# Attention of a hybrid encoder layer with TensorE's order written out: the sink as a column of the score tile, outputs in a PSUM bank of their own, memory rows in two tiles

## The chip, the cores and the metric

The kernel runs on one core of a Trainium2 chip. The core has five engines that each work through a queue of their own in order: TensorE (PE, matmuls; its weight loads appear as a row of their own, PEld), VectorE (DVE), ScalarE (ACT), GpSimd (POOL) and SyncE (SP, which here only issues DMAs). Matmul results go to PSUM, eight banks of 512 fp32 columns on 128 partitions; everything else is in SBUF. The metric is the device time in microseconds (us) of one execution, the median of several runs.

## The reference

One layer of a hybrid encoder, 1024 tokens, model width 1024, all in fp32. One projection of the normalised input feeds a windowed attention and a state-space branch (SSD); both are projected back, weighted by sigmoid gates, summed and projected once more; a cross-attention into 256 memory rows and a squared-ReLU MLP follow.

```python
def reference(x, mem, ...):
    h = rmsnorm(x, norm_mix)
    proj = h @ w_in                      # q, k, v, z, xbc, dt, gate_a, gate_b
    attn = windowed_gqa_sink(q, k, v, attn_sink)
    ssd = ssd_branch(z, xbc, dt_raw, ...)
    merged = sigmoid(gate_a) * (attn @ w_attn_branch) + sigmoid(gate_b) * (ssd @ w_ssd_branch)
    x = x + merged @ w_out
    h = rmsnorm(x, norm_cross)
    x = x + cross_attention(h, rmsnorm(mem, norm_mem), w_xq, w_xkv, w_xo)
    h = rmsnorm(x, norm_ffn)
    x = x + square(relu(h @ w_up)) @ w_down
    return rmsnorm(x, norm_final)

def windowed_gqa_sink(q, k, v, sink):    # 16 heads of 64 over 4 kv heads, blocks of 128 queries
    # each block sees its own and both neighbouring blocks of keys
    s = einsum('bnqgrd,bnkgd->bngrqk', qb, kw) * d ** -0.5 + bias   # ALiBi, -inf outside |t-s| <= 128
    m = maximum(max(s, axis=-1), sink)
    p = exp(s - m)
    denom = sum(p, axis=-1) + exp(sink - m)
    return einsum('bngrqk,bnkgd->bnqgrd', p / denom, vw)
```

## The kernel before

**Products.** An fp32 operand is split into a high and a low part of a format that PE multiplies faster. A product then takes three matmuls (`mm3`, lines 83, 87 and 88): high by high, high by low, low by high. A weight tile is loaded to `raw` by a DMA on SP, its high part `whi` copied by ACT (L64), its low part `wlo` subtracted by POOL (L67). Where a product's result is itself an operand of the next, ACT copies the high part out of PSUM and DVE subtracts the low one.

**Stages.** `phase0` normalises the rows and projects the memory rows; `ssd_phase` runs to about 904 us; `attn_phase` to 1227 us; `merge_phase` projects both branches, beginning with the last gate block (END_GATE, 15) whose first matmul is `mps` of L83; cross-attention and the MLP follow. In all stages but attention PE runs in the order in which the code issues its matmuls (`manual_schedule`). In `attn_phase` a list scheduler of the framework orders every engine, PE too.

**Attention.** For each of four kv heads (`kv`): a key projection of two heads at once in every second round (`kps`, 48 matmuls of 512 columns), in the first round also the values (`vp`, 192 matmuls of 256 columns, L694 to L708), the query projections (`qps`, two units of 48), then eight query blocks (`qb`). `scores(qb)` (L747 to L775) takes for each of four heads `i` two matmuls (`sps`, L761 and L762) over 256 or 384 keys; DVE adds the bias and keeps the minimum, in `t` and `nm` (L763; scores are held negated). Four short operations on [128, 4] tiles deal with the sink: `nm` is lowered to the negated sink (L765), `es` = `nm` + sink (L766), its exp on ACT (L767), and after the four exps of the scores (L769, which also sum into `den`) `den` + `es` (L771). DVE takes the reciprocal (L772), POOL normalises `t` (L774). `values(qb, t4)` (L777 to L802) turns the normalised scores by PE transposes, 4 for each of two or three key blocks (`pt`, L784), splits them into `ph` on ACT (L787) and `pl` on DVE (L788), and multiplies by the values (`op`, L793 and L794, four or six matmuls). ACT copies both halves out (`oa` L797, `ob` L798), POOL adds them (L799), SP stores the sum to `d_at` (L801). `scores` is issued two blocks ahead of `values`. After the blocks of a kv head its gate blocks (`gps`, `ATT_GATES`, numbers 11 to 14) are issued.

**PSUM.** From attention on there are two banks for the projections (tag `g`, pool `pg2`) and six (tag `p`, pool `pp6`) that `vp`, `sps`, `pt` and `op` share in turn.

**Phase 0, memory rows.** PE turns the two groups of 128 memory rows in two halves each (`nt`, L189); DVE multiplies each half by the norm's gain into one tile `mT` (L191); the key products `kxp` (L207) and value products read `mT`. The gain spread over the partitions (`gb`, two matmuls) stands ahead of the transposes.

Of the kernel before, what the change touches and what calls it, by code (L numbers as in the profile page):

```python
# [16 lines left out]
P = 128  # L17
S = 1024
D = 1024
NT = 8  # L20
# [9 lines left out]
ATT_GATES = ((), (11,), (12,), (13, 14))  # L30
# [132 lines left out]
def phase0(kx, ins, dr):  # L163
    nc, tc = kx.nc, kx.tc
    V, A, PE = nc.vector, nc.scalar, nc.tensor
    with tc.tile_pool(name="p0", bufs=1, side="right") as p0, tc.manual_schedule(engines={mybir.EngineType.PE}):
# [15 lines left out]
        mT = p0.tile([P, NK, 256], F32, name="mT")  # L182

        def mem_turn(xt, off):
            for kh in range(2):
                ps = kx.pp.tile([P, 512], F32, tag="p", name="nt")
                for j in range(4):
                    k = 4 * kh + j
                    PE.transpose(ps[:, j * P:(j + 1) * P], xt[:, k * P:(k + 1) * P], kx.ident)  # L189
                to = mT[:, 4 * kh:4 * kh + 4, off:off + P]  # L190
                turned = V.tensor_tensor(to, ps.rearrange("p (k c) -> p k c", k=4),  # L191
                                         gm[:, 4 * kh:4 * kh + 4].unsqueeze(2).broadcast_to([P, 4, P]), ALU.mult)
# [10 lines left out]
        def kx_unit(w, j):  # L203
            ps = kx.pp.tile([P, 512], F32, tag="p", name="kxp")[:, :256]
            wv = w.rearrange("p (k c) -> p k c", k=NK)
            for k in range(NK):
                PE.matmul(ps, wv[:, k], mT[:, k], start=k == 0, stop=k == NK - 1)  # L207
# [4 lines left out]
        def vx_unit(ws, c, j):  # L212
            ps = kx.pp.tile([P, 512], F32, tag="p", name="vxp")[:, :256]
            for k in range(NK):
                wv = ws[k // 4].rearrange("p (k c) -> p k c", k=4)
                PE.matmul(ps, mT[:, k, j * P:(j + 1) * P], wv[:, k % 4], start=k == 0, stop=k == NK - 1)
# [459 lines left out]
def attn_phase(kx, ins, dr):  # L676
    nc, tc = kx.nc, kx.tc
    V, A, G, PE = nc.vector, nc.scalar, nc.gpsimd, nc.tensor
    with tc.tile_pool(name="p2", bufs=1) as ap, tc.tile_pool(name="p2r", bufs=1, side="right") as aq:
# [8 lines left out]
        snk = ap.tile([P, 2, 16], F32, name="snk")  # L688
        nc.sync.dma_start(snk[:, 0], ins["sink"].partition_broadcast(P))
        V.tensor_scalar(snk[:, 1], snk[:, 0], -1.0, None, ALU.mult)  # L690

        vhl = ap.tile([P, NT, 4, 2, 64], F32R, name="vhl")

        def v_part():  # L694
            vw = [wload(kx, ins["wv"][kh]) for kh in range(2)]
            vws = wsplit(vw[0], 4) + wsplit(vw[1], 4)
            for b in range(4):
                vp = kx.pp.tile([P, 512], F32, tag="p", name="vp")
                for j in range(2):
                    t = 2 * b + j  # L700
                    for k in range(NK):
                        mm3(kx, vp[:, j * 256:(j + 1) * 256],
                            act_pair(kx.hT[t // 4], k, slice((t % 4) * P, (t % 4) * P + P)),
                            vws[k], k == 0, k == NK - 1)
                vv = slice(2 * b, 2 * b + 2)
                vp2 = vp.rearrange("p (c v q) -> p c v q", c=2, v=4)
                A.activation(vhl[:, vv, :, 0], vp2, AF.Copy)
                V.tensor_tensor(vhl[:, vv, :, 1], vp2, vhl[:, vv, :, 0].bitcast(F32), ALU.subtract)  # L708

        kd = {}  # L710
        for kv in range(4):
            if kv % 2 == 0:
                w = wload(kx, ins["wk"][kv // 2])
                for s in range(2):
                    kd[kv + s] = [aq.tile([P, S], F32R, tag=n, bufs=2, name=n) for n in ("kh", "kl")]
                for h in range(2):
                    ps = kx.pg.tile([P, 512], F32, tag="g", name="kps")
                    gemm_fm(kx, ps, w, kx.hT[h])
                    hs = slice(h * 512, (h + 1) * 512)
                    for s in range(2):  # L720
                        kh, kl = (t[:, hs] for t in kd[kv + s])
                        own, oth = slice(64 * s, 64 * s + 64), slice(64 - 64 * s, 128 - 64 * s)
                        A.activation(kh[own], ps[own], AF.Copy)
                        A.activation(kh[oth], ps[own], AF.Copy)
                        V.tensor_tensor(kl[own], ps[own], kh[own].bitcast(F32), ALU.subtract)
                        V.tensor_tensor(kl[oth], ps[own], kh[own].bitcast(F32), ALU.subtract)
            if kv == 0:
                v_part()
            qs, bias = [], []
            for i in range(4):  # L730
                bt = ap.tile([P, 384], F32, tag="bias", bufs=5, name="bias")
                A.activation(bt, rel, AF.Copy, scale=SLOPES[4 * kv + i])
                bias.append(bt)
            for i in range(2):
                w = wload(kx, ins["wq"][2 * kv + i])
                q2 = [aq.tile([P, S], F32R, tag="q", bufs=6, name="q") for _ in range(2)]
                for h in range(2):
                    ps = kx.pg.tile([P, 512], F32, tag="g", name="qps")
                    gemm_fm(kx, ps, w, kx.hT[h])
                    for s in range(2):  # L740
                        q = q2[s][:, h * 512:(h + 1) * 512]
                        own, oth = slice(64 * s, 64 * s + 64), slice(64 - 64 * s, 128 - 64 * s)
                        A.activation(q[own], ps[own], AF.Copy, scale=-0.125)
# [1042 lines left out]
```

## Time and profile before

| | |
|---|---|
| time, median of 3 runs | 2340.3 us (2335.47 to 2341.06) |
| the profiled execution | 2340.79 us, its span 2339.0 us |
| granted TensorE clock | 1.0 |
| PE busy over the span | 2301.7 us, 98% |
| PEld, DVE, ACT, POOL busy | 1939.9, 1615.7, 1157.3, 936.8 us |
| bytes moved | 251.04 MB, mean 107 GB/s |

The profile is of one execution. A group of instructions is written as line, engine, operation, output<-inputs. "Idle before" or a wait is time in which an engine had nothing to run, put down to the instruction that released it. A matmul's recorded duration covers its way through the array and overlaps the next matmul's; the distance between two starts is what it costs. PEld rows are the loads of the stationary operand, one for each matmul, which run ahead of the matmuls.

### The profile page before, as it was taken

The numbers are of one execution on the slowest core, as the hardware profiler recorded it, in microseconds if no ns is written. First come the engines' busy times: TensorE is split into PE (matmuls) and PEld (weight loads), VectorE is DVE, ScalarE is ACT, GpSimd is POOL, SyncE is SP. The second block draws the span as 40 slices with busy tenths as digits, with TensorE's granted clock in tenths as the row PEclk, the third lists the DMA queues.
The fourth block names the chain that finished last, engine by engine and source line by source line (L and its number), as shares of the span: only waits on it lengthen the run. The fifth ranks groups of instructions, "written<-read, shape, count | busy, mean of one in ns | idle before, by whom it ended". The sixth has DMA issues, their size and how long they took to land.

```text
span 2339.0 us, 32557 instructions
## 1 busy us (share of the span) xinstructions
PE 2301.7 (98%) x11882; PEld 1939.9 (83%) x11882; DVE 1615.7 (69%) x2578; ACT 1157.3 (49%) x2486; POOL 936.8 (40%) x884
## 2 busy tenths in 40 slices
PE   9999999999999999999999999999999999999998
PEld 7888898988889898877878888888977887788887
DVE  5877666677766764565569887866585456689984
ACT  5455654656555564586775442345453333134342
POOL 2355746566474654453550011115585444100010
PEclk9999999999999999999999999999999999999999
DMA  6222324232242322111135257112353345812301
GB/s 231 83 81 91 116 67 125 71 110 85 79 125 66 118 81 83 44 40 54 37 116 209 82 181 260 46 35 66 128 172 120 108 140 168 297 76 89 119 28 72
DMA packets 150322, 251.04 MB, mean 107 GB/s; under 512 B 11409, under 2 KB 86289, under 8 KB 150162
## 3 DMA queue, kind: packets, MB, share of 16 engines
q1 hardware_dynamic: 79408, 210.41, 26.5%
q10 hardware_dynamic: 70754, 38.55, 5.7%
q8 instruction: 94, 1.54, 0.3%
q14 instruction: 66, 0.54, 0.1%
HBM read 201.47 MB, written 47.45 MB: 106 GB/s over the span
## 4 chain that ended last, share of the span: by engine, by line
PE 81%; DVE 6%; ACT 5%; POOL 3%; issue 3%; DMA 2%; ACTq 0%; POOLq 0%; SPq 0%; DVEq 0%
PE mps L1526 10%; PE dps L1526 10%; PE pb L1321 6%; PE cps L83 4%; PE cps L88 4%; PE cps L87 4%; PE pc L1321 3%; PE zp L83 2%; PE zp L88 2%; PE zp L87 2%; PE cb L599 2%; PE yo L603 2%; ACT t L769 1%; PE mps L88 1%; PE mps L83 1%
## 5 line engine op out<-in xcount | busy, mean ns | idle before, releaser
L67 POOL TENSOR_TENSOR wlo<-raw,whi 128x1024 fp32r<-128x1024 f32 x96 | 235.4, 2453 | 439.6 <-ACT whi L64 417.6
L1477 ACT ACTIVATE kt<-row 128x512 fp32r<-128x512 f32 x264 | 143.1, 619 | 181.2 <-PE dps L1526 82.8
L1526 PE MATMUL mps<-kt 128*128 128x512 f32 x1008 | 229.5, 389 | 0.0
L1526 PE MATMUL dps<-kt 128*128 128x512 f32 x1008 | 228.6, 389 | 0.0
L1526 PEld LDWEIGHTS dps<-kt 128*128 128x128 f32 x1008 | 189.2, 188 | 39.3
L1526 PEld LDWEIGHTS mps<-kt 128*128 128x128 f32 x1008 | 189.1, 188 | 39.2
L83 PE MATMUL cps<-kt,whi 128*128 128x512 f32 x512 | 215.1, 420 | 0.0
L88 PE MATMUL cps<-kt,wlo 128*128 128x512 f32 x512 | 200.0, 391 | 0.0
L87 PE MATMUL cps<-kt,whi 128*128 128x512 f32 x512 | 199.3, 389 | 0.0
L64 ACT ACTIVATE whi<-raw 128x1024 fp32r<-128x1024 f32 x104 | 109.6, 1054 | 163.0 <-DMA raw<-in_wa_dram 31.7
L1478 DVE TENSOR_TENSOR kt<-row,kt 128x512 fp32r<-128x512 f32 x264 | 171.2, 697 | 4.0 <-ACT kt L1477 3.9
L541 POOL TENSOR_TENSOR xl<-xs,xh 128x512 fp32r<-128x512 f32 (+1 forms) x64 | 86.1, 1346 | 105.2 <-ACT xh L540 80.6
L122 POOL TENSOR_TENSOR rr<-rv,mhalf 128x1 f32<-128x1 f32 (+1 forms) x49 | 34.6, 706 | 225.4 <-DVE rv L120 223.5
L1267 POOL TENSOR_TENSOR wop<-w,wop 128x512 fp32r<-128x512 f32 x64 | 85.4, 1338 | 87.7 <-ACT wop L1266 78.7
L87 PEld LDWEIGHTS cps<-kt,whi 128*128 128x128 f32 x512 | 96.3, 188 | 25.3 <-issue 6.7
L83 PEld LDWEIGHTS cps<-kt,whi 128*128 128x128 f32 x512 | 96.2, 188 | 25.0 <-issue 5.3
L88 PEld LDWEIGHTS cps<-kt,wlo 128*128 128x128 f32 x512 | 96.1, 188 | 20.8
L576 ACT ACTIVATE ef<-rows,ebias 128x128 f32<-128x128 f32 x256 | 90.6, 393 | 32.4 <-PE cb L599 29.6
L577 ACT ACTIVATE eb<-rows,ebias 128x128 f32<-128x128 f32 x256 | 89.2, 393 | 34.2 <-POOL rows L569 34.2
L1206 POOL TENSOR_TENSOR wd<-row,wd 128x1024 fp32r<-128x1024 f32 x4 | 11.5, 2878 | 228.3 <-ACT wd L1205 228.3
L83 PE MATMUL gps<-kt,whi 128*128 128x512 f32 x240 | 102.6, 428 | 0.0
L1321 PE MATMUL pb<-kt,wop 128*128 128x512 f32 x384 | 93.3, 391 | 2.8 <-ACT c L1375 2.6
(393 smaller groups left out, 6538.6 us busy)
## 6 DMA issues: line engine op xcount, KB each, us to landing
rows<-d_cs ACTq DMA_DIRECT2D x128, 256.0 KB, 3.9
raw<-in_wssd_dram SPq DMA_DIRECT2D x48, 512.0 KB, 3.8
raw<-in_wup_dram SPq DMA_DIRECT2D x40, 512.0 KB, 3.9
d_u<-c SPq DMA_DIRECT2D x64, 256.0 KB, 2.4
row<-in_wdn_dram SPq DMA_DIRECT2D x28, 512.0 KB, 6.5
row<-d_u SPq DMA_DIRECT2D x28, 512.0 KB, 7.0
x<-in_x_dram SPq DMA_DIRECT2D x16, 512.0 KB, 6.2
raw<-in_wg_dram SPq DMA_DIRECT2D x16, 512.0 KB, 3.7
```

Of the source, the lines that this page charges most:

```text
L64: steps = [nc.scalar.activation(hi, raw, AF.Copy)]
L67: steps.append((eng or nc.gpsimd).tensor_tensor(lo, raw, hi.bitcast(F32), ALU.subtract))
L83: i = mm(out, l[0], r[0], start=first, stop=False)
L87: mm(out, l[0], r[1], start=False, stop=False)
L88: mm(out, l[1], r[0], start=False, stop=last)
L541: G.tensor_tensor(xl[:, lo:hi], xf[:, lo:hi], xh[:, lo:hi].bitcast(F32), ALU.subtract)
L576: A.activation(ef[:, h], rows[:, 0, h], AF.Exp, bias=kx.ebias[:, b, j, 0, o:o + 1])
L577: A.activation(eb[:, h], rows[:, 1, h], AF.Exp, bias=kx.ebias[:, b, j, 1, o:o + 1])
L1321: self.kx.nc.tensor.matmul(ps, w[:, i, ks], act[:, k, j], start=start and k == 0 and m == 0, stop=k == 3 and m == 2, skip_group_check=True)
L1477: nc.scalar.activation(t[:, j, 0], src, AF.Copy)
L1478: nc.vector.tensor_tensor(t[:, j, 1], src, t[:, j, 0].bitcast(F32), ALU.subtract)
L1526: self.kx.nc.tensor.matmul(ps[t], lt[:, k, x, ts], rt[:, k, y], start=n in (1, 2, 5) and k == 0 and m == 0, stop=k == 3 and m == 2, skip_g ...
```

## The change

1. **PE's order in attention is written out.** `attn_phase` now runs under `manual_schedule` for PE. Two query units and the first key unit are projected first, then the first two score blocks with the values between them. Then come 32 steps, one for each kv head and query block: the scores of two steps ahead are interleaved with the three groups of transposes of this step, 18 (later about 15) matmuls of a projection that is due later are put behind them, and the step's `op` matmuls end it, from the last key block to the first, the low part ahead of the high one. The projections fed in are the query and key units of later kv heads and then the gate blocks 11 to 14, which no longer stand behind each kv head.
2. **The sink is a column of the score tile.** `t4` has 385 columns; the negated sink is copied behind the scores (DVE), is the start value of the minimum, and the exp with its sum runs over it. L765, L766, L767 and L771 go.
3. **PSUM**: `op` has a bank of its own (tag `o`), five banks stay for tag `p`. Key tiles have three buffers instead of two, query tiles eight instead of six.
4. **Phase 0**: `mT` is two tiles, one for each half of the model width; each `gb` half stands ahead of one group of transposes.

The core of the diff (`q_unit` and `gate_unit` are built like `k_unit`; `v_block` holds the matmuls and copies of `v_part` for one of its four blocks; `turn` is the transposing half of the former `values`):

```diff
-ATT_GATES = ((), (11,), (12,), (13, 14))
+ATT_GATES = (11, 12, 13, 14)
...
-        mT = p0.tile([P, NK, 256], F32, name="mT")
+        mT = [p0.tile([P, 4, 256], F32, name=f"mT{kh}") for kh in range(2)]
...
-        for h in range(2):
-            PE.matmul(gb[:, h * 512:(h + 1) * 512], ones[0:97], gr[:, h * 512:(h + 1) * 512], start=True, stop=True)
...
         for j in range(2):
+            gs = slice(j * 512, j * 512 + 512)
+            PE.matmul(gb[:, gs], ones[0:97], gr[:, gs], start=True, stop=True)
             turned = mem_turn(xm[j], j * P)
...
-    with tc.tile_pool(name="p2", bufs=1) as ap, tc.tile_pool(name="p2r", bufs=1, side="right") as aq:
+    with tc.tile_pool(name="p2", bufs=1) as ap, tc.tile_pool(name="p2r", bufs=1, side="right") as aq, \
+            tc.manual_schedule(engines={mybir.EngineType.PE}):
...
+        def projected(w, name, evict):
+            for h in range(2):
+                ps = kx.pg.tile([P, 512], F32, tag="g", name=name)
+                ws = wsplit(w)
+                for k in range(NK):
+                    mm3(kx, ps, ws[k], act_pair(kx.hT[h], k), k == 0, k == NK - 1)
+                    if k == NK - 1:
+                        evict(h, ps)
+                    yield
...
-                t4 = ap.tile([P, 4, 384], F32, tag="t4", bufs=3, name="t4")
...
-                V.tensor_tensor(nm, nm, snk[:, 1, 4 * kv:4 * kv + 4], ALU.min)
-                V.tensor_tensor(es, nm, snk[:, 0, 4 * kv:4 * kv + 4], ALU.add)
-                A.activation(es, es, AF.Exp)
...
-                V.tensor_tensor(den, den, es, ALU.add)
...
+            t4 = ap.tile([P, 4, 385], F32, tag="t4", bufs=3, name="t4")
+            sink = snk[:, 4 * kv:4 * kv + 4]
+            V.tensor_copy(t4[:, :, n], sink)
+            for i in range(4):
+                q = qs[kv, i][0]
+                sp_ = kx.pp.tile([P, 512], F32, tag="p", bufs=5, name="sps")
+                PE.matmul(sp_[:, :n], q[:, ql], kh[:, keys], start=True, stop=False)
+                PE.matmul(sp_[:, :n], q[:, ql], kl[:, keys], start=False, stop=True)
+                V.tensor_tensor_reduce(t4[:, i, :n], sp_[:, :n], bias[i][:, bo:bo + n], 1.0, sink[:, i:i + 1],
+                                       ALU.add, ALU.min, accum_out=nm[:, i:i + 1])
+                yield
+            for i in range(4):
+                A.activation(t4[:, i, :n + 1], t4[:, i, :n + 1], AF.Exp, scale=-1.0, bias=nm[:, i:i + 1],
+                             accum_out=den[:, i:i + 1])
...
+        def values(kv, qb, pts):
+            kb0, nb = span(qb)
+            op = kx.pp.tile([P, 512], F32, tag="o", bufs=1, name="op")
+            for kb in range(nb - 1, -1, -1):
+                v2 = vhl[:, kb0 + kb, kv].rearrange("p s q -> p (s q)")
+                PE.matmul(op, v2, pts[kb][1], start=kb == nb - 1, stop=False)
+                PE.matmul(op, v2, pts[kb][0], start=False, stop=kb == 0)
...
+        def feed():
+            nxt = q_unit(1, 0)
+            after = [(q_unit, 1, 1), (q_unit, 2, 0), (q_unit, 2, 1), (k_unit, 2), (q_unit, 3, 0), (q_unit, 3, 1)]
+            after += [(gate_unit, m) for m in ATT_GATES]
+            while nxt:
+                unit = nxt
+                nxt = None
+                for n, _ in enumerate(unit):
+                    if n == 3 and after:
+                        f, *a = after.pop(0)
+                        nxt = f(*a)
+                    yield
+
+        units = [q_unit(0, 0), k_unit(0), q_unit(0, 1)]
+        for u in units:
+            run(u)
+        vws = v_load()
+        slopes(0)
+        t4s = []
+        run(scores(0, 0, t4s))
+        for b in range(2):
+            v_block(vws, b)
+        run(scores(0, 1, t4s))
+        for b in range(2, 4):
+            v_block(vws, b)
+        feeder, fed, steps = feed(), 0, 4 * NT
+        for g in range(steps):
+            kv, qb = divmod(g, NT)
+            ahead = divmod(g + 2, NT)
+            sc = scores(*ahead, t4s) if g + 2 < steps else iter(())
+            t4, pts = t4s.pop(0), []
+            next(sc, None)
+            for kb in range(span(qb)[1]):
+                next(sc, None)
+                pts.append(turn(t4, kb))
+            run(sc)
...
+            due = 6 * (g + 1) if g < 14 else 84 + (92 * (g - 13) + 17) // 18
+            while fed < due:
+                next(feeder, None)
+                fed += 1
+            values(kv, qb, pts)
+        run(feeder)
```

What it moves, at two places. PE in the middle of attention, before: `sps` are the two matmuls of a head's scores, `pt` the transposes, `op` the product with the values, `gps` a gate's projection.

```order
L793 MATMUL op<-ph,vhl 128x512
L761 MATMUL sps<-kh,q 128x384
L762 MATMUL sps<-kl,q 128x384
L794 MATMUL op<-pl,vhl 128x512
L793 MATMUL op<-ph,vhl 128x512
L761 MATMUL sps<-kh,q 128x384
L762 MATMUL sps<-kl,q 128x384
L794 MATMUL op<-pl,vhl 128x512
L793 MATMUL op<-ph,vhl 128x512
```

The six `op` matmuls of a block stand singly between scores, as the scheduler thought them ready. PE in the middle of attention, now (`qps` is a query projection):

```order
L787 MATMUL sps<-kh,q 128x384
L788 MATMUL sps<-kl,q 128x384
L803 MATMUL pt<-ident,t_11232 128x128 x4
L787 MATMUL sps<-kh,q 128x384
L788 MATMUL sps<-kl,q 128x384
L803 MATMUL pt<-ident,t_11232 128x128 x4
L787 MATMUL sps<-kh,q 128x384
L788 MATMUL sps<-kl,q 128x384
L803 MATMUL pt<-ident,t_11232 128x128 x4
L83 MATMUL qps<-kt,whi 128x512
L87 MATMUL qps<-kt,whi 128x512
L88 MATMUL qps<-kt,wlo 128x512
```

The twelve transposes of a block, in a row before, stand in three groups of four between the scores of two blocks on; behind the last group come 18 projection matmuls (the first three are shown), then the block's six `op` matmuls together.

SP at the end of attention, before: `d_at<-oa` are the stores of attention's last blocks, `row` the weight rows (`in_wsb`) and SSD outputs (`d_y`) that merge's first products read.

```order
L801 DMA d_at_0_78<-oa 256x1x128 x4
L1427 DMA row<-in_wsb_dram 128x1024
L1427 DMA row<-d_y_80 128x1024
L1427 DMA row<-in_wsb_dram 128x1024
L1427 DMA row<-d_y_81 128x1024
L801 DMA d_at_1_79<-oa 256x1x128
L1427 DMA row<-in_wsb_dram 128x1024
L1427 DMA row<-d_y_82 128x1024
L801 DMA d_at_1_79<-oa 256x1x128
```

The first four rows for merge stand behind the fourth store from the end. SP at the end of attention, now:

```order
L823 DMA d_at_1_79<-oa 256x1x128
L1490 DMA row<-in_wsb_dram 128x1024
L1490 DMA row<-d_y_80 128x1024
L1490 DMA row<-in_wsb_dram 128x1024
L1490 DMA row<-d_y_81 128x1024
L823 DMA d_at_1_79<-oa 256x1x128
L1490 DMA row<-in_wsb_dram 128x1024
L1490 DMA row<-d_y_82 128x1024
L1490 DMA row<-in_wsb_dram 128x1024
L1490 DMA row<-d_y_83 128x1024
L823 DMA d_at_1_79<-oa 256x1x128
```

They stand one store later, and the last weight rows, 84 to 87, behind the last store.

More of the change, by code (lines that the diff above doesn't have):

```diff
@@ L206, in kx_unit @@
             for k in range(NK):
[L207 removed]
+                PE.matmul(ps, wv[:, k], mT[k // 4][:, k % 4], start=k == 0, stop=k == NK - 1)
             if j == 0:
@@ L687, in attn_phase @@
                         pattern=[[-1, 384]], channel_multiplier=1)
-        snk = ap.tile([P, 2, 16], F32, name="snk")
-        nc.sync.dma_start(snk[:, 0], ins["sink"].partition_broadcast(P))
-        V.tensor_scalar(snk[:, 1], snk[:, 0], -1.0, None, ALU.mult)
+        snk = ap.tile([P, 16], F32, name="snk")
+        nc.sync.dma_start(snk, ins["sink"].partition_broadcast(P))
+        V.tensor_scalar(snk, snk, -1.0, None, ALU.mult)
         vhl = ap.tile([P, NT, 4, 2, 64], F32R, name="vhl")
-        def v_part():
+        kd, qs, bias = {}, {}, {}
@@ L695, in v_part, with v_load @@
+        def v_load():
             vw = [wload(kx, ins["wv"][kh]) for kh in range(2)]
[L696 to L708, printed above, removed]
@@ new lines, in q_unit, with evict @@
+        def q_unit(kv, i):
+            w = wload(kx, ins["wq"][2 * kv + i])
+            def evict(h, ps):
+                for s in range(2):
+                    if h == 0:
+                        qs[kv, 2 * i + s] = aq.tile([P, S], F32R, tag="q", bufs=8, name="q"), sides(s)[0]
+                    q = qs[kv, 2 * i + s][0][:, h * 512:(h + 1) * 512]
+                    own, oth = sides(s)
+                    A.activation(q[own], ps[own], AF.Copy, scale=-0.125)
+                    V.scalar_tensor_tensor(q[oth], ps[own], -0.125, q[own].bitcast(F32), ALU.mult, ALU.subtract)
+            return projected(w, "qps", evict)
@@ new lines, in span, with scores @@
+        def span(qb):
+            kb0, kb1 = max(qb - 1, 0), min(qb + 2, NT)
+            return kb0, kb1 - kb0
+        def scores(kv, qb, t4s):
+            kb0, nb = span(qb)
+            n = nb * P
+            bo = (kb0 - qb + 1) * P
+            ql = slice(qb * P, (qb + 1) * P)
+            keys = slice(kb0 * P, kb0 * P + n)
+            kh, kl = kd[kv]
+            t4 = ap.tile([P, 4, 385], F32, tag="t4", bufs=3, name="t4")
+            nm, den = (ap.tile([P, 4], F32, tag=m, bufs=2, name=m) for m in ("nm", "den"))
+            sink = snk[:, 4 * kv:4 * kv + 4]
[11 more added lines that the diff above has]
+                             accum_out=den[:, i:i + 1])
+            V.reciprocal(den, den)
+            for i in range(4):
+                G.tensor_scalar(t4[:, i, :n], t4[:, i, :n], den[:, i:i + 1], 1.0, ALU.mult, ALU.mult)
+            t4s.append(t4)
@@ new lines, in turn @@
+        def turn(t4, kb):
+            pt = kx.pp.tile([P, 512], F32, tag="p", bufs=5, name="pt")
+            for i in range(4):
+                PE.transpose(pt[:, i * P:(i + 1) * P], t4[:, i, kb * P:(kb + 1) * P], kx.ident)
+            ph = ap.tile([P, 512], F32R, tag="ph", bufs=4, name="ph")
+            pl = ap.tile([P, 512], F32R, tag="pl", bufs=4, name="pl")
+            A.activation(ph, pt, AF.Copy)
+            V.tensor_tensor(pl, pt, ph.bitcast(F32), ALU.subtract)
+            return ph, pl
@@ new lines, in run @@
+        def run(unit):
+            for _ in unit:
+                pass
+        def feed():
[10 more added lines that the diff above has]
+                    yield
```

144 lines of the change are left out of this document (51 added, 93 removed).

## The prediction

> **What bounds the kernel now.** I read the page's totals and its chain first, then the engines' busy time by stage, then what TensorE (PE) and its weight loads (PEld) waited for inside the attention stage, and last the single rows there for the pitch at which instructions start. Totals, chain, and two stages (columns: stretch, length, then busy time of PE, PEld, DVE, ACT, POOL, granted clock, DMA share, GB/s):
>
> ```profile
> PE 2301.7 (98%) x11882; PEld 1939.9 (83%) x11882; DVE 1615.7 (69%) x2578; ACT 1157.3 (49%) x2486; POOL 936.8 (40%) x884
> PE 81%; DVE 6%; ACT 5%; POOL 3%; issue 3%; DMA 2%; ACTq 0%; POOLq 0%; SPq 0%; DVEq 0%
> 100.00:900.00 800.00, 797.33 (x4643) 690.01 (x4642) 554.26 (x752) 446.17 (x1066) 476.53 (x470) 1.00 0.31 94
> 902.00:1228.00 326.00, 315.13 (x1674) 261.59 (x1673) 180.13 (x534) 222.72 (x544) 148.46 (x179) 1.00 0.20 60
> ```
>
> PE bounds the program, yet 19% of the chain lies on other engines. In the SSD stage (100 to 900) PE misses 2.7 us of 800; in the stretch with attention it misses 10.9 us of 326, more than in any other part of such length. ACT, DVE and POOL are at 0.68, 0.55 and 0.46 there: none of them is the bound over the stage. The clock is 1.00, so no time comes from it.
>
> The waits in 900 to 1240, PE's own and those of its weight loads (total us, times, longest):
>
> ```profile
> PE op L794 <- DVE pl L788: 2.7, 5, 1.2
> PE qps L83 <- DVE kl L726: 1.4, 1, 1.4
> PE op L793 <- ACT ph L787: 1.4, 4, 0.5
> PE sps L761 <- DVE nm L763: 0.9, 1, 0.9
> PE pt L784 <- POOL t L774: 0.5, 2, 0.2
> PEld op L793 <- ACT ph L787: 8.7, 19, 0.9
> PEld pt L784 <- POOL t L774: 6.3, 20, 0.6
> PEld op L794 <- DVE pl L788: 5.5, 12, 1.4
> PEld sps L761 <- DVE nm L763: 3.2, 7, 1.2
> ```
>
> The same four causes stand in both lists, all inside attention: 5.5 us by PE's account without the one `qps` wait (6.9 with it), 23.7 us by the weight loads'. Which account is right decides the size of the gain. A matmul's recorded duration is longer than the distance to the next one's start, so PE can look busy while it starves. I therefore count starts.
>
> The stage's ends are its first matmul and the first of the END_GATE block that follows it (start, duration):
>
> ```profile
> 904.54 0.50 PE L83 MATMUL kps<-kt,whi 128*128 128x512 f32 x1 [0.84 <-ACT gt L477]
> 1227.18 0.39 PE L83 MATMUL mps<-kt,whi 128*128 128x512 f32 x1
> 1238.22 152.37 PE mps L1526 x672
> L83 PE MATMUL vp<-whi,kt x64: 278/283/283, 917.8 to 940.4; 128*128 128x256 f32 x64
> 1021.29 0.34 PE L761 MATMUL sps<-kh,q 128*128 128x384 f32 x1
> 1022.86 0.33 PE L762 MATMUL sps<-kl,q 128*128 128x384 f32 x1
> 980.00 1.47 PE L784 MATMUL pt<-ident,t 128*128 128x128 f32 x12
> 981.23 0.48 PE L83 MATMUL qps<-kt,whi 128*128 128x512 f32 x1
> 981.54 0.40 PE L87 MATMUL qps<-kt,whi 128*128 128x512 f32 x1
> ```
>
> So attention lasts 1227.18 − 904.54 = 322.6 us. The pitches: 512 columns 152.37 / 672 = 0.227 us; 256 columns (917.8 to 940.4, 63 triples) 22.6 / 189 = 0.12; 384 columns (ten `sps` in a row, nine steps) 1.57 / 9 = 0.174; a transpose 1.23 / 12 = 0.1025, and the matmul behind the group starts its successor 0.31 later instead of 0.227, so a group of transposes costs 0.085 more. The work, by counts that the code fixes: 848 matmuls of 512 columns (672 projection, 176 `op`) × 0.227 = 192.5; 192 `vp` × 0.12 = 23.0; `sps` 192 × 0.174 + 64 × 0.12 = 41.1; 352 transposes × 0.1025 = 36.1; in before's order they stand in 55 groups × 0.085 = 4.7; the last `yt` groups of SSD in the stretch 0.9. Sum 298.3, so PE starved for about 24.3 us, close to the weight loads' 23.7. I take that as the stock to win from; PE's own 6.9 us is the lower bound.
>
> Here the Trainium skill, "Perfetto Trace Analysis", section "Identifying the Most-Contended Engine", says that TensorE's matmul share is a bad measure of utilisation because matmuls overlap, and that the weight-load share is a better one. The trace agrees: 315.13 against 261.59 us in the same 326. By the page's rule the 23.7 us would be winnable, by PE's own account 6.9.
>
> **The change, part by part.** *The written order in attention.* How much starving remains in a stage whose PE order is written out is shown by SSD, whose rounds repeat exactly:
>
> ```profile
> 206.87 1.75 PE tm L509 x16
> 308.64 1.75 PE tm L509 x16
> L787 ACT ACTIVATE ph<-pt x88: 571/598/629, 972.3 to 1216.6; 128x512 fp32r<-128x512 f32 x88
> L788 DVE TENSOR_TENSOR pl<-pt,ph x88: 673/681/692, 972.9 to 1217.6; 128x512 fp32r<-128x512 f32 x88
> L763 DVE CUSTOM_DVE_ANT_0 t<-sps,bias x128: 407/550/558, 963.0 to 1205.0; 128x384 f32<-128x384 f32 x96, 128x256 f32<-128x256 f32 x32
> L743 ACT ACTIVATE q<-qps x32: 589/593/596, 946.5 to 1172.7; 64x512 fp32r<-64x512 f32 x32
> L797 ACT ACTIVATE oa<-op x32: 582/592/595, 977.4 to 1219.2; 64x512 f32<-64x512 f32 x32
> 978.69 2.40 ACT t L769 x8
> 1203.62 2.27 POOL L774 TENSOR_SCALAR t<-t,den 128x384 f32<-128x384 f32 x4
> 1058.17 0.50 PE L794 MATMUL op<-pl,vhl 128*128 128x512 f32 x1 [1.16 <-DVE pl L788]
> ```
>
> A round there is 101.77 us and PE's busy share 99.7%: a written order can leave next to nothing. Whether this one does follows from one middle step of the new loop. PE: 8 `sps` 1.4, 12 transposes in three groups 1.5, 18 projection matmuls 4.1, 6 `op` 1.4, together 8.4 us (7.7 with 15 projection matmuls, as in the later steps). ACT: four exps 2.4, three `ph` 1.8, `oa` and `ob` 1.2, about 1.5 for `q` evictions and weight splits: 6.9. DVE: four score reductions with their accumulator reads 2.5, three `pl` 2.0, `q` about 1.0, the rest 0.5: 6.0. POOL: normalising 2.3, `oa` sum about 1.3, weight splits about 0.9: 4.5. All fit under 8.4 and, more tightly for ACT, 7.7.
>
> The waits within a step, in time from its first `sps`: the third transposes end at 2.9; ACT has three `ph` at about 3.7; DVE, which has the fourth reduction ahead of the last `pl`, ends it at about 5.0. The first `op` wants it at 7.0 (6.3 with 15 fed), so 1.3 to 2 us of cover lie there: the 18 projection matmuls. Without that cover the wait would be the one in the last row above, 1.16 us, in every step. The exps end at about 6.8, the normalising at 9.3, and the transposes that read it start one step later, at 17: covered by a whole step. The third group of transposes needs a `p` bank whose reduction ends at 1.7, and is due at 2.4. The single `o` bank is free again when `ob` has been copied, 1.3 us after the last `op`; the next `op` is 7 us away. So in steady state I expect no stall; for the first steps, the steps with a `k` eviction (four more copies on ACT, four more on DVE) and the two-block steps at the ends of each head group I allow 3 us in all (bounds 0, and 12 if a third of the steps lose 1.16).
>
> It costs on PE: 85 groups of transposes instead of 55, 30 × 0.085 = 2.6 us. Moving the gates 11 to 14 from behind each head group into the steps leaves their matmul count alone. Attention after: 298.3 + 2.6 + 3 = 303.9, a gain of 18.7 us; upper bound 24.3 − 2.6 = 21.7.
>
> *The sink as a column.* Three small DVE operations and one of ACT go per step, one DVE copy comes:
>
> ```profile
> 1199.03 0.15 DVE L766 TENSOR_TENSOR es<-nm,snk 128x4 f32<-128x4 f32 x1
> 1199.77 0.21 ACT L767 ACTIVATE es<-es 128x4 f32<-128x4 f32 x1
> ```
>
> That is 32 × (3 − 1) × 0.15 = 9.6 us of DVE and 32 × 0.21 = 6.7 of ACT, on engines that are not the bound, and about 0.5 us off a chain that has a step of slack in the new order. The exp and its row grow by one column of 385, which I cost at 385/384 of the exp row, nothing. I book zero, between 0 and −1 (where it shortens a ramp). The output tile's own bank, five `p` banks instead of six, three `kd` and eight `q` buffers cost nothing while the step above holds; the extra buffers are what lets the next projections be written early.
>
> *The edge to merge.* On SP the last four stores of `d_at` now stand ahead of the weight rows of merge's first product, which before were issued from between earlier stores:
>
> ```profile
> 1205.00:1240.00 35.00, 34.37 (x164) 27.70 (x164) 21.87 (x42) 21.21 (x46) 10.14 (x14) 1.00 0.91 311
> 1204.27 0.55 SPq L1427 DMA_DIRECT2D row<-in_wsb_dram  x1
> 1224.54 2.29 SPq L1427 DMA_DIRECT2D row<-in_wsb_dram  x3
> DMA to landing us min/median/max: 3.7/6.1/9.4
> 1238.06 2.23 PE L1526 MATMUL mps<-kt 128*128 128x512 f32 x9
> ```
>
> Let E be the END_GATE block's first matmul (1227.18 before). The first rows were issued at E − 23, four of the eight weight rows by E − 10, the rest from E − 2.6. Now the first pairs go at about E − 14 and E − 8, and the last four weight rows behind the store of the last step, whose `op` ends at E, `ob` at E + 1.3, the sum on POOL at E + 2.7: issue at E + 3.3, landing (3.7 to 9.4 later) E + 7 to E + 13. The product starts at E + 10.9, with the early rows; the late ones are wanted from about E + 13 after a split on ACT and DVE (0.6 and 0.7 each, as `ph` and `pl` of the same shape). DMA is at 0.91 in these 35 us, so landings may be at the late end. A stall of 0 to 3 us; I take 1. Rows of `d_y` 84 and 85 go early in both.
>
> *Phase 0.* The memory rows in two tiles, and each half of the `gb` product moved between the transposes:
>
> ```profile
> 9.11 3.72 PE L207 MATMUL kxp<-mT,w 128*128 128x256 f32 x16 [1.42 <-DVE mT L191]
> ```
>
> At most this 1.42 us goes, if the first four of `kxp` can start after two of the four `mT` products; DVE then holds back the rest, and nothing shows whether `w` was there sooner. Between 0 and −1.4 (a `gb` half adds 0.23 ahead of a transpose: +0.2); I take −0.3.
>
> **Sum.** −18.7 + 1 − 0.3 = −18.0 us against the profiled execution (2340.8 us with a span of 2339.0); that execution lies 0.5 above the median of the three runs, 2340.3. From the median: 2322.3, I say 2322 us (−0.8%).
>
> **Rivals.**
> A. *Only PE's recorded idle is winnable.* PE's 315.13 busy of 326 speaks for it, and of its 6.9 us, 5.5 are attention's stalls. Then −6.9 + 2.6 + 1 with 2 us of new stalls leaves −1.3: 2339, no change that can be told. Against it stand the pitches, which come to the weight loads' number independently.
>
> B. *The new order stalls a little in each step.* Blocks of transposes that PE now must take in turn, five banks, an `op` that begins with the last `pl`: 0.4 us × 32 = 13 us eaten of the gain, 2335. ACT at 6.9 of 7.7 in the later steps speaks for it, the 1.3 us of cover against it. The Trainium skill, "Perfetto Trace Analysis", section "Optimization Strategy", takes regular bubbles as a sign of too little buffer space in SBUF or PSUM; no run here shows yet whether one bank less makes them.
>
> C. *Slower, by one wait: the first `op` on the last `pl`.* If ACT takes the third `ph` only after the four exps of the scores that stand beside it, `ph` ends at 3.7 + 2.4 and `pl` at 6.9 or later, with a `q` eviction between them 1.3 beyond: 8.2 against 7.0 or 6.3. Stalls of 1.2 to 1.9 us; from (18.0 + 7) / 32 = 0.78 us per step on, the kernel is slower by more than 0.3%; at 1.2 it gives 2322 + 38 − 3 = 2357 (the 3 us allowed above are in it). DVE's order, which has the last reduction ahead of that `pl`, leads to this only if ACT's exps come first, and they wait for the same reduction: unlikely.
>
> D. *The two-tile `mT` does nothing*, since PE waited in it for parts before already: 2322.6, inside the first case.
>
> **How the numbers follow.** A gain that beats 0.3% (7 us, about what a measurement of this kernel can tell from no change) needs a time below 2333.3. The forecast with its bounds (residual stalls 0 to 10) 0.80; A 0.08; B 0.08, half of it under 2333; C and a merge stall many times too large 0.04. Faster 0.84, same 0.12, slower 0.04. Range: low end 2340.3 − 21.7 − 0.7 = 2317.9, less the 4.8 us by which the lowest of the three runs, 2335.5, lies under the median: 2313. High end: B's 2335 and a little, 2336, which leaves A and C out.
>
> **What would show it.** In the profile after: attention from its first projection to END_GATE in 302 to 308 us; the weight loads' waits on `ph`, `pl`, `t` down from 23.7 to under 5 us; a step of 7.7 to 8.4 us; no line of PE waiting on a `p` bank; first product of merge 10.9 to 13 us after END_GATE; DVE and ACT some 10 and 7 us less busy. I am wrong if the `op` on the last `pl` or the transposes on `t` show a wait of 0.4 us or more in most steps, or if attention shrinks by the recorded idle alone.

## The result and the profile after

The changed kernel takes 2322.05 us (median of 6 runs, 2320.02 to 2323.7) against 2339.98 us before (6 runs): a ratio of 0.9924, 95% interval 0.9914 to 0.9934. The forecast was 2322 in a range of 2313 to 2336. The total came out as forecast; two of its terms did not, and the experiments show that they were the interesting ones.

Totals and chain of the changed kernel, then, from 895 to 1240 us, where it does attention, all waits of PE itself and three of its weight loads' (total us, times, longest):

```profile
PE 2295.9 (99%) x11882; PEld 1945.0 (84%) x11882; DVE 1606.1 (69%) x2514; ACT 1154.2 (50%) x2454; POOL 935.2 (40%) x884
PE 86%; DVE 5%; ACT 3%; DMA 2%; POOL 2%; issue 2%; SPq 0%; ACTq 0%; POOLq 0%; DVEq 0%
...
PE yt L633 <- ACT yz L625: 0.9, 1, 0.9
PE qps L83 <- ACT gt L477: 0.8, 1, 0.8
PE qps L83 <- DVE kl L739: 0.6, 1, 0.6
PE cb L599 <- DVE ef L585: 0.5, 1, 0.5
...
PEld pt L803 <- DVE nm L789: 1.0, 3, 0.5
PEld op L815 <- DVE pl L807: 0.8, 2, 0.5
...
PEld sps L787 <- DVE nm L789: 0.6, 2, 0.3
```

Of the four causes that held up the weight loads for 23.7 us two are gone and two stand at 1.4 (`op` on `pl`, `sps` on `nm`); the transposes' wait for a bank (`pt` on `nm`) is new, 1.0. The chain has 86% on PE instead of 81. PE's own busy time *fell*, by 5.8 us with the same 11882 matmuls, which fits a PE that looks busier in the records where it starves a little.

The ends of attention and of merge's first part (start, duration):

```profile
908.22 0.50 PE L83 MATMUL qps<-kt,whi 128*128 128x512 f32 x1 [0.84 <-ACT gt L477]
1211.39 0.39 PE L83 MATMUL mps<-kt,whi 128*128 128x512 f32 x1
1222.29 17.92 PE L1589 MATMUL mps<-kt 128*128 128x512 f32 x78
```

Attention lasts 303.17 us, 19.47 less than before; the first product of merge follows END_GATE after 10.90 us, as before (10.88). But attention begins 3.68 us *later* than before, and the loss is in phase 0. What follows merge's start took 1110.4 us instead of 1111.8. These make −19.5 + 3.7 − 1.4 = −17.2 us, the difference of the two spans.

The loss in phase 0 (first the four `mT` products in the kernel before, then in the changed kernel DVE's rows, ACT's row ahead of the `rv` among them, PE's row, and the stretch 12 to 18 us with its granted clock, 0.72):

```profile
7.17 2.48 DVE L191 TENSOR_TENSOR mT<-nt,gm 128x512 f32<-128x512 f32 x4
...
7.02 1.29 DVE L191 TENSOR_TENSOR mT<-nt,gm 128x512 f32<-128x512 f32 x2
10.96 0.15 DVE L120 TENSOR_SCALAR rv<-rss 128x1 f32<-128x1 f32 x1 [2.65 <-ACT xn L129]
11.03 1.28 DVE L191 TENSOR_TENSOR mT<-nt,gm 128x512 f32<-128x512 f32 x2
...
9.78 1.06 ACT L129 ACTIVATE xn<-x 128x1024 f32<-128x1024 f32 x1 [2.88 <-DMA x<-in_x_dram]
...
11.77 5.41 PE L207 MATMUL kxp<-mT,w 128*128 128x256 f32 x16 [2.13 <-DVE mT L191]
...
12.00:18.00 6.00, 6.00 (x23) 5.03 (x23) 3.24 (x6) 1.49 (x3) 0.55 (x1) 0.72 1.03 409
```

Before, the four products ran in a row. Now DVE has a short operation of the token rows' norm (`rv`) between the second and the third. It waits for ACT, which waits for token rows from memory, and the last two `mT` wait behind it. PE idles 2.13 us, and then runs slower: 16 `kxp` in 5.41 us instead of 3.72.

### The profile page after: what moved, and what is told of

The parts are those of the page before. It is cut to its first block, busy times and chain, and to the rows that moved or that the text cites. A ratio compares the mean times of both kernels' runs of the same rounds, so it can differ in the third digit from the quotient of the medians.

```text
span 2321.8 us, 32408 instructions
## 1 busy us (share of the span) xinstructions
PE 2295.9 (99%) x11882; PEld 1945.0 (84%) x11882; DVE 1606.1 (69%) x2514; ACT 1154.2 (50%) x2454; POOL 935.2 (40%) x884
## 4 chain that ended last, share of the span: by engine, by line
PE 86%; DVE 5%; ACT 3%; DMA 2%; POOL 2%; issue 2%; SPq 0%; ACTq 0%; POOLq 0%; DVEq 0%
PE mps L1589 10%; PE dps L1589 10%; PE pb L1384 6%; PE cps L88 4%; PE cps L83 4%; PE cps L87 4%; PE pc L1384 3%; PE zp L83 2%; PE zp L88 2%; PE zp L87 2%; PE cb L599 2%; PE yo L603 2%; PE gps L83 2%; PE gps L87 2%; PE gps L88 2%
## 5 line engine op out<-in xcount | busy, mean ns | idle before, releaser
L789 DVE CUSTOM_DVE_ANT_0 t<-sps,bias,snk 128x384 f32<-128x384 f32 (+1 forms) x128 | 71.5, 582 | 52.4 <-PE sps L788 51.7
L797 POOL TENSOR_SCALAR t<-t,den 128x384 f32<-128x384 f32 (+1 forms) x128 | 69.2, 561 | 90.3 <-DVE den L795 81.2
```

## The experiments

**Phase 0: which part, and what it costs.** The `gb` halves between the transposes moved `rv` in DVE's order. The changed kernel with them put back:

```diff
+        for h in range(2):
+            PE.matmul(gb[:, h * 512:(h + 1) * 512], ones[0:97], gr[:, h * 512:(h + 1) * 512], start=True, stop=True)
         rm = [norm_stats(kx, p0, xm[j], p0.tile([P, D], F32, tag="xn0", bufs=3, name="xn0")) for j in range(2)]
         for j in range(2):
-            gs = slice(j * 512, j * 512 + 512)
-            PE.matmul(gb[:, gs], ones[0:97], gr[:, gs], start=True, stop=True)
             turned = mem_turn(xm[j], j * P)
```

> The changed kernel with both halves of the gain product `gb` put back ahead of the transposes of the memory rows (the memory rows stay in two tiles). In the changed kernel DVE has a short operation of the token rows' norm (`rv`, L120) between the second and the third `mT` product; it waits for ACT, which waits for a transfer of token rows. Theory: that place in DVE's queue cost about 4 us at the program's start (attention began 3.7 us later than before), so this kernel takes 2318 us (2317 to 2319), `kxp` starts at about 9.1 us and the first 16 `kxp` last 3.7 us instead of 5.4. Rival: the transfer was late in that one execution by chance; then this kernel takes 2322 us like the changed one.

And the kernel before with the two edits of phase 0 alone:

> The kernel before with nothing but the change in phase 0 (two `mT` tiles, `gb` halves between the transposes). Theory: 4 us slower than before, about 2344 us, with `kxp` starting at about 11.8 us. Rival, that phase 0's edit is neutral as the prediction had it: 2340 us.

The first took 2320.42 us (0.9916 of before, 0.9903 to 0.993), 1.6 below the changed kernel and above the 2317 to 2319 expected; the second 2345.75 (1.0022, 1.0013 to 1.0032), 5.5 above before. The first `kxp` of each:

```profile
9.98 3.72 PE L207 MATMUL kxp<-mT,w 128*128 128x256 f32 x16
...
11.69 6.74 PE L207 MATMUL kxp<-mT,w 128*128 128x256 f32 x16 [1.51 <-DVE mT L191]
```

The start of attention, in one profiled execution of each, sorts all kernels of this case by that one edit: with the halves ahead it lies at 903.7 to 905.8 us (four kernels, before among them), with the halves between at 906.2 to 911.1 (ten). The means are 904.6 and 908.4, so the edit costs about 3.8 us. How much of it the first kernel's time gives back is not settled by that run (its interval overlaps the changed kernel's): there the transposes ran at about half their pace in the profiled execution (16 in 3.48 us, before in 1.91), for a reason that its rows don't show.

**Order or sink column.** The kernel before with everything but the order and phase 0, that is with the column, the banks and the buffers (an excerpt):

```diff
-                t4 = ap.tile([P, 4, 384], F32, tag="t4", bufs=3, name="t4")
+                t4 = ap.tile([P, 4, 385], F32, tag="t4", bufs=3, name="t4")
...
+                sink = snk[:, 4 * kv:4 * kv + 4]
+                V.tensor_copy(t4[:, :, n], sink)
...
-                op = kx.pp.tile([P, 512], F32, tag="p", name="op")
+                op = kx.pp.tile([P, 512], F32, tag="o", bufs=1, name="op")
```

and the changed kernel with the old sink (an excerpt):

```diff
-            sink = snk[:, 4 * kv:4 * kv + 4]
-            V.tensor_copy(t4[:, :, n], sink)
...
+            V.tensor_tensor(nm, nm, snk[:, 1, 4 * kv:4 * kv + 4], ALU.min)
+            V.tensor_tensor(es, nm, snk[:, 0, 4 * kv:4 * kv + 4], ALU.add)
+            A.activation(es, es, AF.Exp)
             for i in range(4):
...
+            V.tensor_tensor(den, den, es, ALU.add)
             V.reciprocal(den, den)
```

> The kernel before with the sink as a column of the score tile, the output tile in a bank of its own, five banks for the rest, three key and eight query buffers; the order of the code, the gates' places and phase 0 are those of before. Theory: the written order is what won, these parts move the time by 0 to -4 us: 2336 to 2340 us, and the weight loads still wait about 20 us in attention. Rival: the shorter chain and the own bank made the gain; then about 2325 us or less.

> The changed kernel with the sink handled as before (three short DVE operations and one short exp per step instead of a column); order, banks and phase 0 are those of the changed kernel. Theory: the removed operations lie on engines with time to spare and on a chain with a whole step of slack: 2322 us, within 2 us. Rival: the sink column carries part of the gain: about 0.5 us in each of 32 steps, so 2330 to 2338 us.

All but the order: 2332.95 us (0.9969, 0.9958 to 0.9981), attention 314.4 us, 8.3 less than before. The new order with the old sink: 2340.51 us (0.9999, 0.9991 to 1.0008), attention 318.4, only 4.2 less than before, and the loss in phase 0 takes that away. Each alone wins a part, both together 19.5: my theory that the order won fell, and so did the rival that the shorter chain and the own bank did. The new order with the old sink lies above even its rival's range (2330 to 2338 us). In the new order the old sink costs 15.2 us of attention in the profile, which is of the fastest of 11 executions; by the medians it costs 18.5. The 15.2 lie in few steps: two of the 32 lose 5.4 and 4.6 us, three others 1.1 to 1.5. The worst one, in DVE, POOL, PE, and the stretch behind it with PE's granted clock at 0.56:

```profile
1104.17 3.30 DVE L791 TENSOR_TENSOR nm<-nm,snk 128x4 f32<-128x4 f32 x1
...
1110.14 0.16 DVE L797 TENSOR_TENSOR den<-den,es 128x4 f32<-128x4 f32 x1 [1.29 <-ACT t L795]
...
1103.81 1.29 POOL L824 TENSOR_TENSOR oa<-oa,ob 64x512 f32<-64x512 f32 x1
1105.06 2.39 POOL L67 TENSOR_TENSOR wlo<-raw,whi 128x1024 fp32r<-128x1024 f32 x1
...
1112.31 0.76 PE L806 MATMUL pt<-ident,t 128*128 128x128 f32 x4 [2.79 <-DVE nm L788]
...
1112.30:1116.10 3.80, 3.79 (x12) 3.12 (x13) 3.23 (x9) 2.07 (x6) 3.04 (x5) 0.56 0.00 0
```

A minimum of 128 by 4 numbers, 0.16 us in most steps, lasts 3.30. It begins while POOL sums `oa` and ends 0.02 us after POOL's split of a weight tile, which followed at once. The four exps wait for it; on DVE `den` + `es` and the reciprocal wait for the exps; two of the next step's score reductions stand behind these, they free the banks late, and PE waits 2.79 us for one. Then it runs slower for 3.8 us, its 512-column matmuls starting 0.43 us apart instead of 0.227.

**What in the old sink costs it.** Two operations that change no value, each behind the fourth reduction, with the exps waiting for it, one with two inputs in SBUF and one with one:

```diff
+            V.tensor_tensor(nm, nm, sink, ALU.min)                 # the first
+            V.tensor_scalar(nm, nm, 1.0, None, ALU.mult)           # the second
             for i in range(4):
                 A.activation(t4[:, i, :n + 1], t4[:, i, :n + 1], AF.Exp, scale=-1.0, bias=nm[:, i:i + 1],
```

> The changed kernel with one DVE operation more per step: behind the fourth score reduction nm = min(nm, sink), a [128, 4] operation with both inputs in SBUF that changes no value; the exps wait for it. Theory, from the kernel with the old sink, where this operation took up to 3.30 us and ended with POOL's operations: a DVE operation with two SBUF inputs cannot run while POOL does, holds DVE's queue and with it the score tiles' banks; 4 to 12 us slower than the changed kernel, 2326 to 2334 us, with single operations of 1 to 3 us in the profile. Rival: the old sink was slow because its chain has more links; one link more of 0.16 us costs at most 32 x 0.16 = 5 us where it lies on the path and nothing where a step of slack covers it: 2322 to 2324 us, no operation above 0.3 us.

> The same with an operation of one SBUF input in that place, nm = nm x 1, also [128, 4] and changing no value. Theory (the second SBUF input is what waits for POOL): 2322 us like the changed kernel, within 1.5 us, all operations near 0.16 us. Rival (a link more in the chain): as slow as with two inputs. If an operation with one SBUF input waits for POOL too, some of them last over 1 us here.

They took 2332.94 us (0.9973, 0.9962 to 0.9984) and 2335.61 us (0.9983, 0.9974 to 0.9991); attention 316.2 and 316.4 us, 13 more than in the changed kernel. The added operation of the first, then of the second (shortest, median, longest in ns):

```profile
L792 DVE TENSOR_TENSOR nm<-nm,snk x32: 145/152/3105, 947.1 to 1207.8; 128x4 f32<-128x4 f32 x32
...
L792 DVE TENSOR_SCALAR nm<-nm x32: 152/159/3104, 947.1 to 1208.0; 128x4 f32<-128x4 f32 x32
```

One operation per step is enough for 13 of the 15 us, and one input is held up like two: that half of my theory was wrong. The pair doesn't tell the wait for POOL from the exps' common wait, since both have both. Two more kernels take them apart: the common wait put on ACT, and the DVE operation with a result that nothing reads.

```diff
+            A.activation(nm, nm, AF.Copy)                          # the one
+            V.tensor_tensor(es, nm, sink, ALU.min)                 # the other; es is read by nothing
```

> The changed kernel with the short operation of the two kernels before put on ACT: behind the fourth score reduction ACT copies nm onto itself ([128, 4], no value changes), and the exps wait for it. So the four exps wait together for the fourth reduction, as with the old sink, but DVE has no operation more. The extra operation cost 13 us in attention, of which 10 lie in two steps in which it lasted 3.1 us on DVE while POOL was busy. Theory A (DVE waits for POOL): without it on DVE those two steps run as in the changed kernel, at most the 3 us of the other steps are left: 2322 to 2325 us. Theory B (the four exps start together, behind the last reduction): 2330 to 2336 us.

> The changed kernel with the same short DVE operation of two SBUF inputs in the same place, its result written to a tile that nothing reads: the exps do not wait for it, only what stands behind it on DVE does. Theory A (DVE waits for POOL and holds its queue): some of them last 1 to 3 us, and the score banks come free late; 2325 to 2333 us. Theory B (the exps' common wait): 2322 to 2324 us.

The common wait on ACT: 2326.9 us (0.9944, 0.9932 to 0.9957), between the two ranges; attention 306.7, 3.6 more than in the changed kernel; the two bad steps lose 1.2 and 0.4 us there. The unread operation: 2323.31 us (0.9932, 0.992 to 0.9945), attention 303.3, no more than without it. This was a miss of theory A: only one of its 32 lasts over 0.3 us (0.54). Its rows around the step that was worst:

```profile
1098.24 1.29 POOL L823 TENSOR_TENSOR oa<-oa,ob 64x512 f32<-64x512 f32 x1
1102.58 2.27 POOL L799 TENSOR_SCALAR t<-t,den 128x384 f32<-128x384 f32 x4 [3.04 <-DVE den L797]
...
1101.32 0.16 DVE L793 TENSOR_TENSOR es<-nm,snk 128x4 f32<-128x4 f32 x1
```

Here it falls into 3 us in which POOL is idle, and of the other 31 only the one of 0.54 us meets a POOL operation at all. In the kernel with two inputs it began at 1103.56, with POOL in `oa`; six of its 32 last over 0.3 us, and each of them begins while POOL is at work and ends within 0.03 us of the end of a POOL operation.

The kernel with the common wait on ACT shows more than it was built for. Nothing was added on DVE there, but the copy that the sink column itself needs is held up in the same step (DVE, POOL, ACT):

```profile
1102.28 3.08 DVE L783 COPY t<-snk 128x4 f32<-128x4 f32 x1
...
1101.66 1.29 POOL L822 TENSOR_TENSOR oa<-oa,ob 64x512 f32<-64x512 f32 x1
1102.91 2.42 POOL L67 TENSOR_TENSOR wlo<-raw,whi 128x1024 fp32r<-128x1024 f32 x1
...
1102.64 0.62 ACT L794 ACTIVATE t<-t,nm 128x385 f32<-128x385 f32 x1
```

In the changed kernel the longest of these copies takes 0.81 us. So the exps' common wait, with no operation more on DVE, already brings a short DVE operation and POOL's work together. And DVE's queue is held here as long as by the added operation (3.08 and 3.10 us), yet the step loses 1.2 us and not 5.7: the exps don't wait for the copy. With the added operation they began only at 1106.70, behind its end, and the reciprocal, which waits for them ahead of the next reductions on DVE, at 1109.24. So the common wait alone costs 3.6 us, the operation alone nothing, and the operation as the common wait's link 13, because the exps then stand behind an operation that POOL holds up. One thing is not separated: DVE is still ordered by the scheduler, and in the kernels with the common wait it puts the reciprocal of 5 (wait on ACT), 10, 10 and 12 (old sink) of the 32 steps behind a reduction of the next step, in the changed kernel and in that with the unread operation of none. How much of the 13 us comes from this order no run shows.

**The cover in a step.** The step's `op` ahead of the projection matmuls instead of behind them:

```diff
-            while fed < due:
-                next(feeder, None)
-                fed += 1
             values(kv, qb, pts)
+            while fed < due:
+                next(feeder, None)
+                fed += 1
```

> The changed kernel with a step's `op` matmuls ahead of the projection matmuls instead of behind them, so that nothing covers the copies of the transposed scores. Theory, from the prediction's count of a step: the first `op` then wants the last `pl` at 2.9 us and has it at about 5.0; 1.2 to 2.1 us per step, 38 to 67 us, 2360 to 2389 us, with PE waiting in `op` on `pl` in most steps. Rival: the next step's scores and the other engines catch up, so that a step loses under 0.4 us: below 2335 us.

2422.69 us (1.0351, 1.0337 to 1.0365). Waits of PE, and one stretch with the granted clock at 0.90:

```profile
PE op L815 <- DVE pl L807: 71.3, 31, 4.8
...
1120.00:1180.00 60.00, 45.46 (x218) 37.66 (x217) 31.02 (x86) 38.28 (x90) 21.61 (x28) 0.90 0.10 29
```

The wait is where the prediction put it, and with 2.3 us on average in 31 steps a little longer than the 1.2 to 2.1 expected. The total, 100 us, is above the 67 expected: the waits make 71 of it, and most of the rest is the clock, which from 1000 to 1240 us was granted at 0.90 to 0.91 (240 × 0.095, about 23 us).

**Transposes in one row**, with `gb` ahead:

```diff
-            next(sc, None)
+            for _ in range(3):
+                next(sc, None)
             for kb in range(span(qb)[1]):
-                next(sc, None)
                 pts.append(turn(t4, kb))
```

> The changed kernel with the `gb` halves ahead of the memory rows' transposes (2320.4 us alone) and with a step's transposes in one row, between the third and the fourth head's scores: 31 groups instead of 85. Theory, from the price of a group in the trace of before: 54 x 0.085 = 4.6 us faster than with the `gb` halves alone, 2316 us (2314 to 2318). Rival: three transposed tiles in a row want three of the five shared banks at once; PE then waits 0.2 us or more per step for a bank, and the time is 2320 us or more.

2319.61 us (0.9912, 0.9898 to 0.9925), the fastest kernel here, but within the spread of the one with `gb` ahead (2320.42); attention 302.5 us, only 0.8 less than there. That is above the 2314 to 2318 expected, yet PE has no wait for a bank in attention that took the gain; there was none to have. A group of four in the changed kernel, and one of twelve here, each with the two matmuls behind it:

```profile
1010.86 0.60 PE L803 MATMUL pt<-ident,t 128*128 128x128 f32 x4
1011.21 0.36 PE L787 MATMUL sps<-kh,q 128*128 128x256 f32 x1
1011.41 0.28 PE L788 MATMUL sps<-kl,q 128*128 128x256 f32 x1
...
1007.17 1.47 PE L803 MATMUL pt<-ident,t 128*128 128x128 f32 x12
1008.40 0.36 PE L787 MATMUL sps<-kh,q 128*128 128x256 f32 x1
1008.61 0.28 PE L788 MATMUL sps<-kl,q 128*128 128x256 f32 x1
```

Four take 0.35 and the matmul behind them 0.08 more than its 0.12: 3 × 0.43 = 1.29. Twelve take 1.23, and 0.09: 1.32. The change of the group costs 0.08 each time, but the transposes of a short group are nearer together, which the prediction did not see.

**Banks and scheduler.** The output tile among six shared banks, and the changed kernel without the fixed order:

```diff
-            op = kx.pp.tile([P, 512], F32, tag="o", bufs=1, name="op")
+            op = kx.pp.tile([P, 512], F32, tag="p", bufs=6, name="op")     # the one; 6 for sps, pt and vp too
...
-    with tc.tile_pool(name="p2", bufs=1) as ap, tc.tile_pool(name="p2r", bufs=1, side="right") as aq, \
-            tc.manual_schedule(engines={mybir.EngineType.PE}):
+    with tc.tile_pool(name="p2", bufs=1) as ap, tc.tile_pool(name="p2r", bufs=1, side="right") as aq:   # the other
```

> The changed kernel with the output tile among the six banks that scores, transposes and outputs share, instead of a bank of its own beside five. Theory, since no wait for a bank is left in the changed kernel: 2322 us, within 2 us. Rival: the own bank is what lets outputs and scores run without waiting for each other; then 2326 us or more, with PE waiting in `sps` or `pt` on `ob`.

> The changed kernel with PE's order in attention left to the framework's list scheduler as before; the code is written in the new order. The scheduler leaves the steps as they are written but for the start, where it puts half a query projection behind the first scores, two steps in which it puts one projection matmul ahead of a group of transposes, and nothing else that matters. Theory: what moves the time is the order in which the code is written, not who fixes it: 2322 us, within 2 us. Rival: the fixed order itself is needed; 2326 us or more.

2323.55 us (0.9924, 0.991 to 0.9938; attention 302.8) and 2322.82 us (0.9928, 0.9916 to 0.994; attention 302.5): both as expected. The bank of its own is worth nothing that these runs can tell, and neither is fixing PE's order. What counts is the order in which the code is written, since the scheduler keeps it nearly whole.

## Why the prediction was right, and where it was not

- **The stock to win.** The pitches gave 24.3 us of starving, the weight loads 23.7, PE's own idle 6.9. Attention came out at 303.2 us (303.9 forecast), 19.5 less: the weight loads' account was the right one, and rival A is out. Two errors nearly cancel in that forecast: the 2.6 us for more groups of transposes did not exist (twelve in a row or three times four: 1.32 and 1.29 us), and 303.2 − 298.3 = 4.9 us are left over the work where 3 were allowed. The section of the Trainium skill that the prediction cites there ("Perfetto Trace Analysis", "Identifying the Most-Contended Engine") speaks of the loads' share of the time; that the sum of their waits tells what can be won was a step of mine.
- **The step.** A full middle step took 8.24 us with 18 fed (8.4 forecast) and 7.57 with 15 (7.7). The cover of the last `pl` by the projection matmuls held (weight loads wait 0.8 us in all), and without it the forecast wait appears. Rivals B and C did not happen.
- **The sink column: the step that failed.** "I book zero, between 0 and −1." In the new order it is worth 15.2 us of attention (318.4 against 303.2). The price of 0.15 us that I took for each of its operations was one row's. All 32 of each in the kernel before read:

```profile
L765 DVE TENSOR_TENSOR nm<-nm,snk x32: 129/161/1203, 966.7 to 1205.8; 128x4 f32<-128x4 f32 x32
...
L766 DVE TENSOR_TENSOR es<-nm,snk x32: 138/156/1201, 967.4 to 1206.0; 128x4 f32<-128x4 f32 x32
...
L771 DVE TENSOR_TENSOR den<-den,es x32: 152/164/1091, 969.1 to 1210.4; 128x4 f32<-128x4 f32 x32
```

  A longest of 1.2 us where the median is 0.16 was there to be read: something holds these operations up. It is POOL: 16 of the 96 begin while it sums `oa` or splits a weight tile, and each of them ends within 0.06 us of that operation's end, while 13 score reductions ran wholly inside such operations at their usual length. And the removed ones were a joint: with the column each head's exp waits for its own reduction alone, before all four waited for the fourth. "A chain that has a step of slack" missed that the chain's end, the sum and the reciprocal, stands in DVE's queue ahead of reductions, and so holds PSUM banks that PE wants within the step. The gain of 18.7 us that I gave the order was the gain of both; the order without the column wins 4.2. Had the change come without the column, the same forecast would have been wrong by 18 us (2340.5). That the total was right is in this part luck.
- **Phase 0: sign wrong.** −0.3 forecast, about +3.8 measured. I priced the wait that might go and the `gb` half that moves, and did not look at what stands between the `mT` products on DVE in the new order. The row was in the order of the changed kernel: an operation that waits for a transfer, now ahead of two on which PE waits.
- **Merge.** 0 instead of +1. The last weight rows were issued 3.4 us behind END_GATE (3.3 forecast), ACT then waited for two of them (1.4 and 1.1 us), and the products had 10.90 us of other work to cover it.
- **The rest.** DVE is 9.6 us less busy (9.6 forecast), ACT 3.1 (6.7 forecast): the exps with one column more, put at nothing, took 614 ns where they took 603 (medians of 128).

The Trainium skill, "SBUF — State Buffer", section "Who interferes with whom", states what these traces show: DVE and GpSimd share a pair of SBUF ports as an exclusive lock, and a DVE operation with two SBUF inputs, or a `tensor_scalar` in a two-port mode, is blocked for as long as GpSimd holds it. The 3.30 us above and the 3.10 of both added operations agree, the one-input form included, and so does that reductions and `pl`, with one input in PSUM, never show it (`pl` 673 to 692 ns before). Read against the three rows above, that page would have told what holds these operations up; the 13 us it would not have given, since these hang on what waits for the held operation.

## What to carry to other kernels

Read the longest of a group, not only its median: a tiny operation whose longest is seven times its median is held up by something, and if it joins several chains, what it costs is not its time but what waits for it: a hold of 3.1 us cost a step 5.7 us where four exps waited for it, and 1.2 where they didn't. Price an order by what stands between the producers and the consumers on every engine that feeds the bound one, the short waiting operations above all; and count starts, since a busy matmul engine may be a starving one. Two edits that each win little can win much together, so undo them one at a time in the new kernel, not only add them one at a time to the old.

## What the runs showed of the hardware

A stall of PE can cost more than its length. In the kernel without cover 12 of its waits were followed by matmuls at 0.43 us instead of 0.227, for 2.5 to 6 us; the shortest such wait was 1.95 us, while others of up to 2.7 us were not followed by it, and in attention before, where the longest wait was 1.4 us, none was. The Trainium skill, "TensorE: Matmul & The Clock Gate", section "What's actually happening", puts the halving behind an idle window of about 3.4 us that runs free; the half clock agrees, and so does that waits of one length are followed by it at some times and not at others, but here idle times well under 3.4 us were enough.
